# A hybrid decoder layer on one core: the second stage's three-term products regrouped over four tiles, the block sums stored in another order, and 24 stores issued from GpSimd's queue

## The chip, the core and the metric

The kernel runs on one NeuronCore of one Trainium2 chip. A core has TensorE (matmul, PE in the profile; PEld is its weight load), VectorE (DVE), ScalarE (ACT), GpSimd (POOL) and SyncE (SP). SP and POOL here mainly issue DMAs: each keeps its DMAs in one order, and a DMA that has to wait for something holds up every DMA behind it on the same engine. The metric is the device time of one execution in microseconds, median over several runs; less is better. One execution is profiled, and its trace gives every instruction with its start, its length and what it waited for.

## The reference, cut to what matters

The input x is (1, 2048, 1024) in f32, and there is one layer. The first part (projection, two groups of recurrent heads) is not touched by the change; the second part is the output projection, a norm and the feed-forward network:

```python
h = _rmsnorm(x, norm1_w[l])
proj = h @ w_in[l]
...
x = x + jnp.concatenate([o_hg, o_rw], axis=-1) @ w_out[l]
x = x + _conv_ffn(_rmsnorm(x, norm2_w[l]), w_up[l], conv_w[l], conv_b[l], w_down[l])
...
return _rmsnorm(x, final_norm_w)

def _conv_ffn(h, w_up, conv_w, conv_b, w_down):
    u = h @ w_up                                  # 1024 -> 2 * 2816
    u = <causal depthwise convolution, 3 taps>(u) + conv_b
    gate, val = jnp.split(u, 2, axis=-1)
    return (jax.nn.silu(gate) * val) @ w_down     # 2816 -> 1024
```

## The kernel before

**Three terms for one product.** Every large product is made at near-f32 precision from two halves. `split` (L241 to L248) rounds a tile to its high part on ScalarE (L246, names that end in h) and subtracts to get the low part on VectorE (L247, names that end in l); `split_to` (L239, L240) does the same into given tiles. `mm3` (L259 to L264) then adds three matmuls into one PSUM accumulator: high by high (L262), high by low (L263) and low by high (L264), each 128x128 by 128x512. Their lines tell the three terms apart in the trace. The program's names in a row stand as output, then moving operand, then stationary operand: `ua<-Bh,uwl` is the low part of a weight tile, stationary, with the high part of a B tile streaming through.

**Second stage, in order of time.** It runs from about 1391 us to the end.

1. The last block's output projection. For each half `dh` of the 1024 columns, eight k tiles in the order 0, 1, 4, 5, 2, 3, 6, 7 are multiplied into four accumulators `wacc`, one for each 128 rows. For k tile n, `weights` loads and splits a tile of w_out (names `uraw`, `woh`, `wol`) and `take` loads and splits the tile of the heads' output (into slices of `Bh` and `Bl`); then four `mm3`.
2. The up-projection, `run`. The feature columns are 22 blocks of 128 for gate and for value (`NFF` = 22) and the 2048 positions two halves, so that n goes from 0 to 43. Each n computes a 2x2 block product by Strassen's scheme with seven products; each product (`prod`) is four k tiles by three terms, 12 matmuls. The accumulators are `ua`, `ub` and `ud`, the B operands are seven pairs `Bh[i]`, `Bl[i]` that stay in SBUF for one half, and the weight operands are loaded raw (`uraw`), combined on VectorE (`s`) and split (`uwh`, `uwl`). After n the convolution and the gate are computed on VectorE and ScalarE (`cg`, `cv`, `y`) and the result goes to DRAM tensors `gd` (L1449): to gd_154 and gd_155 for the first half, to gd_156 and gd_157 for the second.
3. One side job after each product. `aside` (one call for each of the seven products of an n) pops a list that was filled ahead: `norm_last` (the norm and the transposes of the last blocks, L1253 and L256), sums of B tiles (`Ts`) and of down weights (`Tw`), and `sums(g, kk)`. `sums` loads four `gd` tiles in four slots of a ring of six (`br`, L1124), combines them with four additions on VectorE (L1293) and stores the four results to `Sg` (L1294). For g = 0 it runs at n = 23 to 33 on gd_154 and gd_155; for g = 1 with kk < 7 it runs at n = 36 to 42 on gd_156 and gd_157, while those tensors are still being written.
4. Between the halves (n = 21 and 22) the seven B pairs are rebuilt for the second half (`rebuild`, `build`), and eleven steps of an independent product (`between`, accumulators `fa`) are placed between the others to keep TensorE fed.
5. The down-projection, again by Strassen: 2 groups g, 7 products p, 11 k steps each. `down_start` does five steps, and the last loop does the others. Step s loads two raw tiles four steps ahead (`draw`, L1462, ring of six), splits them two steps ahead (`dah`, `dal`, `dbh`, `dbl`) and does four `mm3` (`d_matmuls`) into `da` or `db`. At four steps (13, 19, 25 and 31) `g_sums` makes the four sums of g = 1 that `sums` did not make: four loads `sraw`, four operations (L195 to L198), four stores to `Sg` (L201). At the end of a product `evict` adds it to the residual tile, and `finish` scales a finished tile and stores it to the output.

**What sets the order.** The program is written as above, and a tile framework then puts each engine's instructions into an order by its own estimates, with semaphores for the dependences. It follows a DRAM tensor as one object: a load from gd_157 waits for the stores to gd_157 that stand ahead of it, whichever rows they write.

Of the kernel before, what the change touches and what calls it, by code (L numbers as in the profile page):

```python
# [18 lines left out]
P = 128  # L19
T = 2048  # L20
D = 1024
KD = D // P
# [39 lines left out]
def tile_layer(ctx, tc, consts, x, norm1_w, w_in, hg_lb_logits, hg_norm_w, rw_shift_mu, rw_w0, rw_w2,  # L62
# [5 lines left out]
    dma = nc.sync.dma_start  # L68
# [124 lines left out]
    def g_sums(tile_, g, kk):  # L193

        a11, a12, a21, a22 = (tile_(krows(gd_[2 * g + u], q, kk)) for u in range(2) for q in range(2))  # L195
        V.tensor_add(a22, a21, a22)
        V.tensor_sub(a21, a11, a21)
        V.tensor_sub(a11, a22, a11)  # L198
        V.tensor_sub(a12, a12, a11)
        for i, t_ in enumerate((a22, a11, a21, a12)):  # L200
            dma(krows(Sg[g][i], 0, kk), t_)  # L201
# [7 lines left out]
    def d_loads(s_, tile_):  # L209
# [3 lines left out]
                tile_(krows(Tw[b], 0, kk) if isinstance(b, int) else wd_quarter(*b, kk)))  # L213

# [45 lines left out]
    def mm3(acc, lhs, rhs, first, last, skip=False):  # L260
# [3 lines left out]
        TE.matmul(acc, ll, rh, start=False, stop=last, skip_group_check=skip)  # L264

# [843 lines left out]
    with ExitStack() as c2:  # L1109
# [36 lines left out]
        with tc.tile_pool(name="op", bufs=1, reuse_waits="tile") as op_:  # L1146
# [84 lines left out]
        with tc.tile_pool(name="up", bufs=1, reuse_waits="tile") as up:  # L1231
# [11 lines left out]
            def norm_last(b, i2):  # L1243
# [17 lines left out]
                aside_of([load, None, lambda: scale(0), lambda: scale(1), None] + [lambda: next(g)] * KD)  # L1261
# [25 lines left out]
            def sums(g, kk):  # L1287

                ts = []
                ops = ((3, V.tensor_add, 2, 3), (2, V.tensor_sub, 0, 2), (0, V.tensor_sub, 3, 0), (1, V.tensor_sub, 1, 0))  # L1290
# [5 lines left out]
                aside_of([lambda: ts.extend(raw_(krows(gd_[2 * g + u], q, kk)) for u, q in QB), None, None]  # L1296
# [15 lines left out]
            def down_start():  # L1312

                accs = [pst("da") for _ in range(4)]
                for s_ in range(DS):
                    lhs, rhs = (split(uw, t_, [P, BLK], "uw", 5) for t_ in d_loads(s_, raw_))
                    for i in range(4):
                        d_matmuls(accs, s_, lhs, rhs, i)
                dstate["accs"] = accs

            def between():

                accs = [pst("fa") for _ in range(4)]
                for kk in range(KH):
                    lhs, rhs = (split(uw, raw_(v), [P, BLK], "uw", 5)
                                for v in (krows(gd_[0], 1, kk), wd_quarter(1, 0, kk)))
                    for i in range(4):
                        mm3(accs[i], [t_[:, i * P:(i + 1) * P] for t_ in lhs], rhs, kk == 0, kk == KH - 1, True)
# [16 lines left out]
            def run():  # L1345
# [9 lines left out]
                for n in range(2 * NFF + 1):  # L1355
                    h, fb = n // NFF, n % NFF
                    if n < 2 * NFF:
# [7 lines left out]
                        def prod(acc, nm, bi, first, n=n, ops=ops):  # L1365
# [89 lines left out]
    with tc.tile_pool(name="dn", bufs=1, reuse_waits="tile") as dn:  # L1455
# [33 lines left out]
        def finish(g, u, i):  # L1489
# [3 lines left out]
            dma(out[0, t0:t0 + P, :], t_)  # L1493
# [23 lines left out]
        for s_ in range(DS, N):  # L1517
# [6 lines left out]
            if s_ < N - 3:  # L1524
                lhs, rhs = ops.pop(s_)
                for i in range(4):
# [52 lines left out]
```

## Time and profile before

| | |
|---|---|
| median of 3 runs | 2740.66 us (2735.97 to 2741.07) |
| profiled execution | 2734.05 us |
| its span in the trace | 2732.2 us |
| TensorE busy | 2631.2 us, 96% of the span, 18059 matmuls |
| VectorE busy | 1896.6 us, 69% |
| ScalarE busy | 1348.1 us, 49% |
| GpSimd busy | 367.5 us, 13% |
| mean granted TensorE clock | 0.991 |

The profiled execution is 6.6 us faster than the median; the span is what the trace covers, and 1.85 us of the execution lie outside it. A row of a timeline gives the start and the length in us, the engine, the line, the operation, out<-in, the shape, and in brackets the idle time ahead of it with what ended that. Matmuls overlap: one starts 0.227 us after the other though each lasts 0.39, so that a lost stretch shows in the starts or as bracketed idle time. A row of the groups gives the count, then busy time and mean ns of one, then the idle time just ahead with what ended it. A row of the windows gives the length, and for PE, PEld, DVE, ACT and POOL the busy time with the number of instructions, then the granted clock, the DMA engines' busy share and GB/s.

### The profile page before, as it was taken

How to read it: one execution, taken by the hardware profiler on the slowest of the kernel's cores; microseconds unless marked ns; L12 is line 12 of the kernel's file. 1: busy time of each engine (PE TensorE's matmuls, PEld its weight loads, DVE VectorE, ACT ScalarE, POOL GpSimd, SP SyncE). 2: the span in 40 equal slices, each digit the busy share in tenths (PEclk: the TensorE clock that was granted, in tenths of full speed). 3: DMA queues.
4: the chain of work that ended last, by engine and by line, in shares of the span. 5: the costliest groups of instructions: out<-in, count | busy, mean ns of one | idle time of the engine just before them, and what ended most of it. 6: DMA issues, size and time to landing. Idle time of an engine off the chain costs nothing.

```text
span 2732.2 us, 47983 instructions
## 1 busy us (share of the span) xinstructions
PE 2631.2 (96%) x18059; PEld 2097.0 (77%) x18059; DVE 1896.6 (69%) x3665; ACT 1348.1 (49%) x2168; POOL 367.5 (13%) x660
## 2 busy tenths in 40 slices
PE   7989999989999999999899999999999999999998
PEld 5767777767777767777677788887888877788887
DVE  4856656566456654756668789988888888677556
ACT  4546443444544335334456765456555445445444
POOL 6433222212321113222100000000000000000000
PEclk9999999999999999999999999999999999999999
DMA  8655544354663546854576358746655454898665
GB/s 299 198 162 165 171 138 134 115 147 156 215 199 105 138 140 212 280 143 132 165 245 192 119 193 268 234 151 222 222 187 194 132 191 131 287 320 289 213 193 185
DMA packets 365438, 517.88 MB, mean 190 GB/s; under 512 B 97439, under 2 KB 194069, under 8 KB 365205
## 3 DMA queue, kind: packets, MB, share of 16 engines
q1 hardware_dynamic: 313265, 345.39, 39.4%
q0 software_dynamic: 51872, 169.41, 19.2%
q8 instruction: 142, 2.33, 0.4%
q14 instruction: 91, 0.75, 0.1%
q10 hardware_dynamic: 68, 0.02, 0.0%
HBM read 376.27 MB, written 138.41 MB: 188 GB/s over the span
## 4 chain that ended last, share of the span: by engine, by line
PE 68%; DVE 11%; DMA 9%; issue 6%; ACT 4%; SPq 1%; POOL 1%; DVEq 0%; ACTq 0%; POOLq 0%
PE pj L262 8%; PE pj L263 7%; PE pj L264 7%; PE ua L262 4%; PE ua L264 4%; PE ua L263 4%; PE da L262 3%; PE da L263 3%; PE da L264 3%; PE ud L264 2%; PE ud L262 2%; PE ud L263 2%; PE db L263 2%; PE db L262 2%; PE db L264 2%
## 5 line engine op out<-in xcount | busy, mean ns | idle before, releaser
L262 PE MATMUL pj<-hh,wh 128*128 128x512 f32 x960 | 402.7, 420 | 2.2 <-ACT rkv L117 1.1
L263 PE MATMUL pj<-hl,wh 128*128 128x512 f32 x960 | 378.4, 394 | 0.0
L264 PE MATMUL pj<-hh,wl 128*128 128x512 f32 x960 | 378.4, 394 | 0.0
L262 PE MATMUL ua<-Bh,uwh 128*128 128x512 f32 x704 | 276.7, 393 | 7.2 <-ACT m L117 5.6
L264 PE MATMUL ua<-Bh,uwl 128*128 128x512 f32 x704 | 274.4, 390 | 0.0
L263 PE MATMUL ua<-Bl,uwh 128*128 128x512 f32 x704 | 274.2, 389 | 0.0
L262 PEld LDWEIGHTS pj<-hh,wh 128*128 128x128 f32 x960 | 181.0, 189 | 55.6 <-issue 12.2
L264 PEld LDWEIGHTS pj<-hh,wl 128*128 128x128 f32 x960 | 181.0, 189 | 40.1 <-DMA wl<-Win170l 0.6
L263 PEld LDWEIGHTS pj<-hl,wh 128*128 128x128 f32 x960 | 181.4, 189 | 39.1 <-issue 6.2
L246 ACT CAST uwh<-uraw 128x512 fp32r<-128x512 f32 x220 | 134.5, 617 | 139.3 <-PE ua L263 61.8
L247 DVE TENSOR_TENSOR dal<-draw,dah 128x512 fp32r<-128x512 f32 x138 | 95.3, 690 | 112.5 <-ACT dah L246 112.3
L247 DVE TENSOR_TENSOR uwl<-uraw,uwh 128x512 fp32r<-128x512 f32 x220 | 147.1, 686 | 36.3 <-ACT uwh L246 36.3
L246 ACT CAST dah<-draw 128x512 fp32r<-128x512 f32 x138 | 85.8, 622 | 166.2 <-PE da L263 74.5
L262 PEld LDWEIGHTS ua<-Bh,uwh 128*128 128x128 f32 x704 | 132.2, 188 | 37.4 <-ACT m L117 8.9
L264 PEld LDWEIGHTS ua<-Bh,uwl 128*128 128x128 f32 x704 | 132.1, 188 | 28.2 <-DVE uwl L247 0.4
L263 PEld LDWEIGHTS ua<-Bl,uwh 128*128 128x128 f32 x704 | 132.3, 188 | 26.7
L262 PE MATMUL ud<-Bh,uwh 128*128 128x512 f32 x352 | 137.7, 391 | 0.0
L264 PE MATMUL ud<-Bh,uwl 128*128 128x512 f32 x352 | 137.1, 389 | 0.0
L263 PE MATMUL ud<-Bl,uwh 128*128 128x512 f32 x352 | 137.0, 389 | 0.0
L263 PE MATMUL da<-dbl,dah 128*128 128x512 f32 x332 | 129.5, 390 | 0.2 <-DVE dbl L247 0.2
L264 PE MATMUL da<-dbh,dal 128*128 128x512 f32 x332 | 129.2, 389 | 0.0
L1449 POOL DMA_DIRECT2D gd<-y x2 | 1.1, 554 | 952.0 <-DVE y L1447 952.0
(567 smaller groups left out, 6189.3 us busy)
## 6 DMA issues: line engine op xcount, KB each, us to landing
uraw<-in_w_up_dram SPq DMA_DIRECT2D x176, 256.0 KB, 3.3
woraw<-in_w_out_dram POOLq DMA_DIRECT2D x96, 256.0 KB, 3.5
br<-gd SPq DMA_DIRECT2D x88, 256.0 KB, 4.4
draw<-Sg SPq DMA_DIRECT2D x88, 256.0 KB, 3.3
draw<-Tw SPq DMA_DIRECT2D x88, 256.0 KB, 3.4
gd<-y SPq DMA_DIRECT2D x86, 256.0 KB, 2.9
Sg<-br SPq DMA_DIRECT2D x72, 256.0 KB, 2.3
xt<-x1d SPq DMA_DIRECT2D x32, 512.0 KB, 6.5
```

What stands on the lines that cost most here:

```text
L246: S.copy(hi, src)
L247: V.tensor_sub(lo, src, hi.bitcast(F32))
L262: TE.matmul(acc, lh, rh, start=first, stop=False, skip_group_check=skip)
L263: TE.matmul(acc, lh, rl, start=False, stop=False, skip_group_check=skip)
L264: TE.matmul(acc, ll, rh, start=False, stop=last, skip_group_check=skip)
L1449: (dma if end is None else nc.gpsimd.dma_start)(gd_[2 * h + b][fb * P:(fb + 1) * P, :], ys[0][:, b * BLK:(b + 1) * BLK])
```

## The change

Four things change, all in the second stage. The instruction order of all engines is the same in both programs up to the first `wacc` matmul.

**Terms.** A new function does the first term of four tiles, then the second term of the four, then the third:

```diff
+    def terms3(jobs, first, last):
+
+        for j in range(3):
+            for n, (acc, (lh, ll), (rh, rl)) in enumerate(jobs):
+                TE.matmul(acc, *((lh, rh), (lh, rl), (ll, rh))[j], start=first(n) and j == 0, stop=last(n) and j == 2,
+                          skip_group_check=True)
```

It takes the place of four `mm3` in the up products, in `between`, in `down_start`, in the down steps other than the last k step of a product and the last three steps of all, and in the first two k tiles of each half of the output projection:

```diff
-                    for i in range(4):
-                        is_ = slice(i * P, (i + 1) * P)
-                        mm3(accs[i], (ohl[k][0][:, is_], ohl[k][1][:, is_]), w, n == 0, n == KD - 1)
+                    prods = [(accs[i], [t_[:, i * P:(i + 1) * P] for t_ in ohl[k]], w) for i in range(4)]
+                    if n < 2:
+                        terms3(prods, lambda i: n == 0, lambda i: False)
+                    else:
+                        for p_ in prods:
+                            mm3(*p_, False, n == KD - 1, True)
...
-                            for k in range(4):
-                                mm3(acc, (wh[:, k, :], wl[:, k, :]), (bh[:, k, :], bl[:, k, :]),
-                                    first and k == 0, k == 3, True)
+                            terms3([(acc, (wh[:, k, :], wl[:, k, :]), (bh[:, k, :], bl[:, k, :])) for k in range(4)],
+                                   lambda k: first and k == 0, lambda k: k == 3)
...
-                for i in range(4):
-                    d_matmuls(acc, s_, lhs, rhs, i)
-                    if kk == KH - 1:
+                if kk < KH - 1:
+                    d_step(acc, s_, lhs, rhs)
+                else:
+                    for i in range(4):
+                        d_matmuls(acc, s_, lhs, rhs, i)
                         evict(g, p, accs, i)
```

**Sums.** The four tiles are loaded second pair first, and the operations overwrite them in such a way that the results stand in the order in which they are stored. The values are the same sums.

```diff
-                ops = ((3, V.tensor_add, 2, 3), (2, V.tensor_sub, 0, 2), (0, V.tensor_sub, 3, 0), (1, V.tensor_sub, 1, 0))
+                ops = ((1, V.tensor_add, 0, 1), (0, V.tensor_sub, 2, 0), (2, V.tensor_sub, 1, 2), (3, V.tensor_sub, 3, 2))
...
-                aside_of([lambda: ts.extend(raw_(krows(gd_[2 * g + u], q, kk)) for u, q in QB), None, None]
+                aside_of([lambda: ts.extend(raw_(krows(gd_[2 * g + u], q, kk)) for u, q in QB[2:] + QB[:2]), None, None]
```

**The norm's side job** has one more empty slot between the scaling and the transposes:

```diff
-                aside_of([load, None, lambda: scale(0), lambda: scale(1), None] + [lambda: next(g)] * KD)
+                aside_of([load, None, lambda: scale(0), lambda: scale(1), None, None] + [lambda: next(g)] * KD)
```

**Stores.** The 16 stores of `g_sums` and the 8 output stores of g = 0 are issued by GpSimd's queue instead of SP's; the output stores of g = 1 stay on SP:

```diff
+    dma, store = nc.sync.dma_start, nc.gpsimd.dma_start
...
-            dma(krows(Sg[g][i], 0, kk), t_)
+            store(krows(Sg[g][i], 0, kk), t_)
...
-            dma(out[0, t0:t0 + P, :], t_)
+            (dma if g else store)(out[0, t0:t0 + P, :], t_)
```

In the changed program the lines lie further down: a matmul of `terms3` is L275, `split` is at L251 and L252, the load of `raw_` at L1136, the sums at L1308 and L1309, the store to `gd` at L1462, the loads of the down stage at L1475.

**How the order of the instructions moves.** First, SP's DMAs during one n of the sums for g = 1 (n = 36 to 42). gd_156 and gd_157 are the second half's two activation tensors, Sg_162 to Sg_165 the four sums. Before:

```order
L1141 DMA uraw<-in_w_up_dram 128x4x128
L1124 DMA br<-gd_156 128x512
L1124 DMA br<-gd_157 128x512 x2
L1294 DMA Sg_165<-br 128x512
L1124 DMA br<-gd_156 128x512
L1294 DMA Sg_162<-br 128x512
L1294 DMA Sg_164<-br 128x512
L1141 DMA uraw<-in_w_up_dram 128x4x128
L1294 DMA Sg_163<-br 128x512
L1141 DMA uraw<-in_w_up_dram 128x4x128 x2
L1449 DMA gd_156<-y_22370 128x512
L1449 DMA gd_157<-y_22370 128x512
```

and now:

```order
L1153 DMA uraw<-in_w_up_dram 128x4x128
L1136 DMA br<-gd_157 128x512
L1136 DMA br<-gd_156 128x512 x2
L1136 DMA br<-gd_157 128x512
L1309 DMA Sg_162<-br 128x512
L1309 DMA Sg_164<-br 128x512
L1309 DMA Sg_163<-br 128x512
L1309 DMA Sg_165<-br 128x512
L1153 DMA uraw<-in_w_up_dram 128x4x128 x3
L1462 DMA gd_156<-y_22368 128x512
L1462 DMA gd_157<-y_22368 128x512
```

In both lists the first three loads belong to the sums at hand and the fourth is already the first of the next n. The first of the four operations needs the two tiles of gd_157. Before, these were the second and the third load behind the stores to `gd`, and the store of the preceding sums' last tile (Sg_165) stood ahead of the fourth load. Now the one tile of gd_157 has come an n earlier and the other is the first load behind the stores to `gd`; it waits for the store to gd_157, the later of the two, and all four stores of the sums stand behind the loads. Second, VectorE at the same place. Before:

```order
L1421 TENSOR_TENSOR cv<-ud,m_22640 128x512
L1293 TENSOR_TENSOR br<-br 128x512
L1438 COPY cg<-halo 128x2
L1438 COPY cv<-halo 128x2
L247 TENSOR_TENSOR uwl<-s_22754,uwh 128x512
L1293 TENSOR_TENSOR br<-br 128x512 x2
L247 TENSOR_TENSOR uwl<-uraw,uwh 128x512
L1293 TENSOR_TENSOR br<-br 128x512
L1441 SCALAR_TENSOR_TENSOR y_22717<-cv,cvt,y_22717 128x1024
```

and now:

```order
L1434 TENSOR_TENSOR cv<-ud,m_21956 128x512
L1451 COPY cg<-halo 128x2
L1451 COPY cv<-halo 128x2
L252 TENSOR_TENSOR uwl<-s_22068,uwh 128x512
L1308 TENSOR_TENSOR br<-br 128x512 x4
L252 TENSOR_TENSOR uwl<-uraw,uwh 128x512
L1454 SCALAR_TENSOR_TENSOR y_22031<-cv,cvt,y_22031 128x1024
```

The four sums of an n now stand in one piece; before, the last of the preceding n's sums stood ahead of the copies, and the third and last of its own n behind one more split. Third, SP's DMAs around the first `g_sums` of the down stage. Before:

```order
L1462 DMA sraw<-gd_156 128x512 x2
L1462 DMA sraw<-gd_157 128x512 x2
L1462 DMA draw<-Sg_159 128x512
L1462 DMA draw<-Tw_167 128x512
L1477 DMA xt_23623<-x1d_147 128x1024
L201 DMA Sg_162<-sraw 128x512
L201 DMA Sg_163<-sraw 128x512
L201 DMA Sg_164<-sraw 128x512
L201 DMA Sg_165<-sraw 128x512
L1462 DMA draw<-Sg_159 128x512
L1462 DMA draw<-Tw_167 128x512
```

and now:

```order
L1475 DMA sraw<-gd_156 128x512 x2
L1475 DMA sraw<-gd_157 128x512 x2
L1475 DMA draw<-Sg_159 128x512
L1475 DMA draw<-Tw_167 128x512
L1490 DMA xt_23621<-x1d_147 128x1024
L1475 DMA draw<-Sg_159 128x512
L1475 DMA draw<-Tw_167 128x512
```

The next step's two loads no longer stand behind the four stores; the stores are the same four on GpSimd's queue, where only the later `g_sums` stores and the eight output stores follow them.

More of the change, by code (lines that the diff above doesn't have):

```diff
@@ L213, in d_loads, with d_step @@
                 tile_(krows(Tw[b], 0, kk) if isinstance(b, int) else wd_quarter(*b, kk)))
+    def d_step(accs, s_, lhs, rhs):
+        g, p, kk = steps[s_]
+        terms3([(accs[i], [t_[:, i * P:(i + 1) * P] for t_ in lhs], rhs) for i in range(4)],
+               lambda i: kk == 0 and p in (0, 1, 3), lambda i: False)
     def d_matmuls(accs, s_, lhs, rhs, i):
```

8 lines of the change are left out of this document (3 added, 5 removed).

## The prediction

> **What bounds the kernel now.** I read the page's head first, then the groups of instructions by line, then windows of two like stretches, then timelines at the places where TensorE waits.
>
> ```profile
> span 2732.2 us, 47983 instructions
> PE 2631.2 (96%) x18059; PEld 2097.0 (77%) x18059; DVE 1896.6 (69%) x3665; ACT 1348.1 (49%) x2168; POOL 367.5 (13%) x660
> L262 PE MATMUL ua<-Bh,uwh 128*128 128x512 f32 x704 | 276.7, 393 | 7.2 <-ACT m L117 5.6
> L264 PE MATMUL ua<-Bh,uwl 128*128 128x512 f32 x704 | 274.4, 390 | 0.0
> L262 PE MATMUL da<-dbh,dah 128*128 128x512 f32 x332 | 126.0, 390 | 2.4 <-ACT dbh L246 2.4
> L263 PE MATMUL fa<-uwl,uwh 128*128 128x512 f32 x44 | 17.4, 394 | 2.6 <-DVE uwl L247 2.6
> L262 PE MATMUL fa<-uwh 128*128 128x512 f32 x44 | 15.0, 392 | 0.8 <-ACT uwh L246 0.8
> ```
>
> TensorE sets the end. In the second stage its groups stand idle for a few us in all: the up products 7.2 at the first term and nothing at the low parts, the steps between the halves 2.6 and 0.8, the down products 2.4. The change can win these and little else, unless a matmul itself becomes cheaper or dearer. The rate of a dense stretch answers that:
>
> ```profile
> 2499.74 0.39 PE L263 MATMUL db<-dbl,dah 128*128 128x512 f32 x1
> 2499.96 0.39 PE L264 MATMUL db<-dbh,dal 128*128 128x512 f32 x1
> 2500.19 0.39 PE L262 MATMUL db<-dbh,dah 128*128 128x512 f32 x1
> ```
>
> L263 keeps the stationary tile of the matmul ahead of it, L264 takes another, the next L262 another again and a new accumulator as well; the starts are 0.22 and 0.23 us apart all the same, and every matmul has its weight load (18059 of each). The new order changes the stationary tile at every matmul and the accumulator too; at this rate that costs nothing. So the change is worth what its waits are worth, and I take it place by place.
>
> **A, the start of the output projection.** The first k tile's low parts come late.
>
> ```profile
> 1391.48 0.40 PE L262 MATMUL wacc<-woh,Bh 128*128 128x512 f32 x1
> 1393.02 0.50 PE L263 MATMUL wacc<-wol,Bh 128*128 128x512 f32 x1 [1.15 <-DVE wol L240]
> 1394.83 0.50 PE L264 MATMUL wacc<-woh,Bl 128*128 128x512 f32 x1 [1.30 <-DVE Bl L240]
> 1396.12 0.63 PE L262 MATMUL wacc<-woh,Bh 128*128 128x512 f32 x1
> ...
> 1391.00:1395.10 4.10, 1.65 (x6) 0.83 (x5) 4.10 (x7) 0.74 (x2) 0.49 (x1) 1.00 0.71 263
> 1395.10:1399.00 3.90, 3.90 (x11) 3.04 (x11) 0.88 (x2) 0.00 (x0) 0.00 (x0) 0.56 0.93 237
> ...
> 1455.09 0.50 PE L262 MATMUL ua<-Bh,uwh 128*128 128x512 f32 x1 [1.46 <-ACT uwh L246]
> ```
>
> One matmul waits for the low weight, the next for the low part of the other operand (VectorE is busy for all 4.10 us), and behind them nine more of the first k tile are left. In the new order four high matmuls run from 1391.48, four with the low weight from 1393.02, and only four are left at 1394.83. VectorE's order here is the same in both, so these two times stay. Before, ten matmuls of this k tile start at 1394.83 or later (that one and nine behind it), now four: 6 x 0.227 = 1.36 us. In addition the granted clock fell to 0.56 in the next 3.9 us, when eleven matmuls took what seventeen take at 0.227: up to 1.4 us more if the fuller start keeps the clock up. On the other side stands the wait of 1.46 us at the first up product, for a weight tile whose load need not move with it: what arrives there early may wait there longer. Ends 0 and 2.8, I take 1.5.
>
> [...]
>
> **B, the norm's transposes.** One empty slot more moves the transposes of each `norm_last` by one product, 12 x 0.227 = 2.7 us.
>
> ```profile
> 1556.38 0.55 PE L256 MATMUL tp<-ident,xt 128*128 128x128 f32 x3 [0.96 <-DVE xt L1253]
> ```
>
> The tile came 0.96 us too late, so one product hides it whole. No work is added, the tile's two buffers are held 2.7 us longer. Between 0.3 and 1.0; I take 1.0.
>
> **C, between the halves.** Here low parts are late, and the new order does four high matmuls, then the neighbour's four high and two to four low ones, before the first low one of `fa`.
>
> ```profile
> 1865.13 0.50 PE L263 MATMUL fa<-uwl,uwh 128*128 128x512 f32 x1 [1.00 <-DVE uwl L247]
> 1900.80 0.50 PE L263 MATMUL fa<-uwl,uwh 128*128 128x512 f32 x1 [1.62 <-DVE uwl L247]
> ```
>
> Four to six more matmuls of cover are 0.9 to 1.4 us at each of the two, up to 2.4 together, and the 0.8 at the high part is not helped. Against it, a B tile that is to be rebuilt is now read last by the ninth matmul of its product instead of the third: 6 x 0.227 = 1.36 us later for the first k tile, and ScalarE, which rebuilds it, does its work in order, the next split behind it. One or two such delays cancel the gain. From -2 to +2.4; I take 0.7.
>
> **D, the sums of g = 1.** The like stretch of the sums of g = 0 stands first, one n of each.
>
> ```profile
> 2012.30:2031.35 19.05, 19.05 (x86) 15.78 (x85) 17.09 (x26) 9.69 (x14) 0.00 (x0) 1.00 0.59 191
> 2208.61:2229.44 20.83, 19.36 (x84) 15.69 (x84) 17.08 (x26) 9.46 (x16) 0.00 (x0) 1.00 0.54 176
> DVE br L1293 <- DMA br<-gd: 23.9, 8, 3.7
> 2206.20 0.81 SPq L1449 DMA_DIRECT2D gd<-y  x2
> 2208.61 0.38 SPq L1141 DMA_DIRECT2D uraw<-in_w_up_dram  x1
> 2209.09 1.41 SPq L1124 DMA_DIRECT2D br<-gd  x3
> 2215.45 1.42 DVE L1293 TENSOR_TENSOR br<-br 128x512 f32<-128x512 f32 x2 [3.72 <-DMA br<-gd]
> DMA to landing us min/median/max: 2.0/3.8/5.3
> ```
>
> For g = 0 an n takes TensorE's 84 matmuls, 19.05 us; VectorE has 17.09 us of work in it and 1.96 to spare. For g = 1 VectorE has the same work and waits 3.72 us for a load, which is 1.76 more than it has: the n takes 20.83, 1.78 longer. Over the group it waits 23.9 us in 8 waits, 3.0 each, of which about 1.0 is over what it can spare; for seven n that is 7.1 us, near the 7.2 of the up group. This is a stretch where VectorE and a chain of transfers (store of `y`, load, sum) set the pace, not TensorE.
>
> The tile that ends the wait is the third load of the three at 2209.09, issued at about 2210.1, landed 5.3 us later. In the new order the first operation needs the first of the three, which has to follow the store to gd_157, 0.4 us behind the other: issue 2209.5, landing 3.8 at most (the median of loads and stores alike), so 2213.3. The second needs the next load, issued 0.5 us behind and slower than the first; the fourth needs the third. VectorE comes there 0.6 us earlier, at 2211.1, as the preceding n's last sum no longer stands ahead. It waits 2.2 us for the first load and 0.6 to 0.9 more for the second: about 2.8 to 3.1 in place of 3.7. The chain is shortened, not removed, because a load still stands behind the store just issued. 0.6 us for seven n is 4.2; the others' waits are shorter than this one, 3.0 to 3.7, so I take 3.4. Ends: 0, if the loads land as late as before, and 7.1.
>
> **E, the down stage's stores.** The four stores of the first `g_sums` wait for VectorE, and the next loads stand behind them on SP.
>
> ```profile
> 2374.57 0.32 SPq L1477 DMA_DIRECT2D xt<-x1d  x1
> 2378.75 2.98 SPq L201 DMA_DIRECT2D Sg<-sraw  x4
> 2381.84 0.39 SPq L1462 DMA_DIRECT2D draw<-Sg  x1
> 2385.25 0.62 ACT L246 CAST dah<-draw 128x512 fp32r<-128x512 f32 x1 [5.26 <-DMA draw<-Sg]
> 2386.66 1.20 PE L262 MATMUL da<-dbh,dah 128*128 128x512 f32 x4 [2.44 <-ACT dbh L246]
> 2375.98 0.69 DVE L247 TENSOR_TENSOR dbl<-draw,dbh 128x512 fp32r<-128x512 f32 x1
> ```
>
> The pair of loads left at 2381.84, its first tile was split at 2385.25, 3.4 us later, and the matmul started 1.4 after that, 2.44 late. Without the stores ahead, the pair leaves when its ring slots come free, with the split that ends at 2376.7: five us earlier. Even at the 5.3 that a slow load took above, the matmul's operands are there at 2376.7 + 5.3 + 1.4 = 2383.4, and TensorE is free at 2384.2. So the whole 2.4 goes; the other three `g_sums` show no such wait, and the group's 2.4 says the same. On GpSimd's queue the stores delay nothing, since it has nothing else to do in this stage, and the `Sg` tiles they write are first read over 60 steps of 12 matmuls later. The eight output stores of g = 0 are taken from SP where TensorE waits for nothing: 0. Ends 1.5 and 2.4.
>
> **Sum.** 1.5 + 1.0 + 0.7 + 3.4 + 2.4 = 9.0 us off the profiled execution: 2734.05 - 9.0 = 2725.1. That execution lies 6.6 us under the median of the runs shown, so off the median: 2740.66 - 9.0 = 2731.7 us.
>
> **Rivals.** What a measurement here can tell from no change is 0.2%, 5.5 us.
>
> 1. *The gains stay short of the end.* A is used up at the wait of 1455.09, the loads of D land no earlier since they still follow the store, and C's cover is paid back by the rebuilds. B and E stay: 3.4 us, 2737.3. For it: D's chain of store and load is still there. Against: the first load of three now decides, not the third.
> 2. *D's wait goes below what VectorE can spare.* Then the 7.1 comes whole: 9.0 - 3.4 + 7.1 = 12.7, 2728.0. For it: the median landing of 3.8. Against: three loads together took up to 5.3.
> 3. *The sums in one piece make VectorE the bound for g = 0 too.* Four sums in a row stop VectorE until the last tile is there, and all splits behind them stop as well. If its wait there became the 3.0 of g = 1, each of the eleven n would take 17.09 + 3.0 = 20.1 in place of 19.05: 11.4 us, and D would give nothing. It decides from a wait of 1.96 us per n. Sum: 11.4 - 5.6 = 5.8 us slower, 2746.5. Against: gd_154 and gd_155 are finished then, so no load stands behind a fresh store, and all the waits of the row are eight, as many as g = 1 needs alone.
>
> **How the numbers follow.** The forecast has 0.48, rival 1 0.26, rival 2 0.14, rival 3 0.12. The forecast's own range is 2728 to 2735. The range of 8 in 10 reaches to rival 2 with the spread of the runs below it (2722) and over rival 1 to near the median before and a little past it (2743), with most of rival 3 left out. Faster by over 5.5 us: nearly all of rival 2, 0.13, and nine tenths of the forecast, 0.43, and a little of rival 1, 0.02: 0.58. Slower by over 5.5: half of rival 3 and mishaps in C, 0.10. Within: 0.32.
>
> **What would show it.** A: the second k tile's first matmul 1.4 to 2.8 us earlier, and the granted clock of 1395 to 1399 near 1. B: no idle time at L256. C: the groups of `fa` idle for under 2 us in all. D: the windows of n = 36 to 42 nearer 20.2 than 20.8, VectorE's wait at L1308 near 2.4 on average and ended by two loads, and no wait there for g = 0. E: the group `da` idle 0. The forecast is wrong if the dense starts move from 0.227 us, if idle time appears in g = 0, or if a first up product waits longer by what A won.

## The result, and the profile after

The changed kernel takes 2732.29 us in the median of 22 runs (2717.2 to 2740.99), the kernel before 2739.46 us in 22 runs beside it (2731.65 to 2753.36). The ratio is 0.9966, with a 95% interval of 0.9953 to 0.9979: faster by 0.34%, 9 us (the two medians alone are 7.2 apart). The forecast was 2731.7 us, and 9.0 us less than before.

The head of the page of the changed kernel, and its groups by line that answer to those of before (count | busy us, mean ns | idle time ahead of the group and what ended it):

```profile
span 2728.8 us, 47991 instructions
PE 2633.8 (97%) x18059; PEld 2098.7 (77%) x18059; DVE 1898.3 (70%) x3665; ACT 1357.3 (50%) x2166; POOL 380.4 (14%) x684
L275 PE MATMUL ua<-Bh,uwh 128*128 128x512 f32 x704 | 191.5, 394 | 6.6 <-ACT m L117 6.3 <-ACT uwh L251 0.3
L275 PE MATMUL da<-dbh,dah 128*128 128x512 f32 x300 | 81.7, 390 | 0.0
L261 PE MATMUL tp<-ident,xt 128*128 128x128 f32 x64 | 12.2, 272 | 0.0
L275 PE MATMUL fa<-uwl,uwh 128*128 128x512 f32 x44 | 12.0, 395 | 2.8 <-DVE uwl L252 2.8
L275 PE MATMUL fa<-uwh 128*128 128x512 f32 x44 | 11.9, 392 | 2.1 <-ACT uwh L251 2.1
```

The mean length of a matmul has not moved (389 to 395 ns), as the dense stretch had said. The idle time of the down group (`da`, 2.4 before) and of the transposes (`tp`, 1.0) is gone. That of the groups between the halves (`fa`) has grown from 3.4 to 4.9, and the up group still waits 6.6 us, 6.3 of them for `m`, ScalarE's copy of an accumulator. So something that made that group wait is gone and something else has come.

Totals hide this, and one execution hides more: the first stage, with the same instructions in the same order, took 1380.6 us in the profile of before and 1368.7 to 1386.7 in those of the experiments. So I cut the second stage at fixed matmuls and compare place by place. The times are the distances between the starts of the first matmuls of these places: "n = 12 to 19" runs from the first `ub` matmul of n = 12 to that of n = 20, "down 1" takes 1200 matmuls from the 61st of `da` on, the output projection and "n = 0 to 2" meet at the first `ua` matmul, and the whole ends with the start of the last matmul. Each kernel was profiled twice (the second time with only a comment changed):

| place | before | before, again | changed | changed, again |
|---|---|---|---|---|
| first stage | 1380.6 | 1385.2 | 1381.8 | 1386.7 |
| output projection | 48.4 | 49.7 | 46.4 | 46.9 |
| n = 0 to 2 | 63.9 | 62.1 | 64.1 | 64.8 |
| n = 3 to 11 (transposes) | 178.9 | 178.7 | 177.9 | 177.4 |
| n = 12 to 19 (down-weight sums) | 152.7 | 152.9 | 157.3 | 156.7 |
| n = 20 to 23 (between the halves) | 110.4 | 114.2 | 111.9 | 112.1 |
| n = 24 to 34 | 209.4 | 209.4 | 209.4 | 209.4 |
| n = 35 to 42 (sums of g = 1) | 159.8 | 160.1 | 155.5 | 154.2 |
| n = 43 and the first five down steps | 30.1 | 30.1 | 30.0 | 30.0 |
| down 1 | 276.1 | 278.7 | 272.9 | 272.8 |
| rest of the down stage | 103.1 | 103.1 | 103.2 | 103.2 |
| second stage in all | 1332.9 | 1339.0 | 1328.5 | 1327.5 |

The mean of the second stage falls from 1335.9 to 1328.0, by 7.9 us, near the 9 that were timed. Four places win, as forecast. One loses 4.2 us that the prediction did not have at all, and n = 0 to 2 is longer by 1.4.

### The profile page after: what moved, and what is told of

The parts are those of the page before. It is cut to its first block, busy times and chain, and to the rows that moved or that the text cites. A ratio compares the mean times of both kernels' runs of the same rounds, so it can differ in the third digit from the quotient of the medians.

```text
span 2728.8 us, 47991 instructions
## 1 busy us (share of the span) xinstructions
PE 2633.8 (97%) x18059; PEld 2098.7 (77%) x18059; DVE 1898.3 (70%) x3665; ACT 1357.3 (50%) x2166; POOL 380.4 (14%) x684
## 4 chain that ended last, share of the span: by engine, by line
PE 72%; DMA 8%; DVE 8%; issue 6%; ACT 4%; SPq 1%; POOL 1%; DVEq 0%; ACTq 0%; POOLq 0%
PE ua L275 14%; PE pj L267 8%; PE pj L268 7%; PE pj L269 7%; PE da L275 7%; PE ud L275 7%; PE db L275 5%; PE ub L275 3%; PE hg L985 2%; DMA woraw<-in_w_out_dram 1%; PE rw L721 1%; DVE uwl L252 1%; DMA TZ<-T0d 1%; PE rw L901 1%; DVE y L1454 1%
## 5 line engine op out<-in xcount | busy, mean ns | idle before, releaser
L275 PE MATMUL ua<-Bh,uwh 128*128 128x512 f32 x704 | 191.5, 394 | 6.6 <-ACT m L117 6.3
L275 PE MATMUL ua<-Bl,uwh 128*128 128x512 f32 x704 | 188.4, 389 | 0.0
L275 PE MATMUL ua<-Bh,uwl 128*128 128x512 f32 x704 | 188.4, 389 | 0.0
L251 ACT CAST uwh<-uraw 128x512 fp32r<-128x512 f32 x220 | 134.1, 617 | 92.2 <-PE ua L275 62.7
L252 DVE TENSOR_TENSOR dal<-draw,dah 128x512 fp32r<-128x512 f32 x138 | 95.3, 690 | 110.1 <-PE da L275 50.8
L252 DVE TENSOR_TENSOR uwl<-uraw,uwh 128x512 fp32r<-128x512 f32 x220 | 147.6, 687 | 33.7 <-PE ua L275 19.2
L275 PEld LDWEIGHTS ua<-Bh,uwh 128*128 128x128 f32 x704 | 129.9, 188 | 37.0 <-ACT m L117 10.8
L251 ACT CAST dah<-draw 128x512 fp32r<-128x512 f32 x138 | 85.7, 621 | 138.2 <-PE da L275 51.7
L275 PEld LDWEIGHTS ua<-Bl,uwh 128*128 128x128 f32 x704 | 132.1, 188 | 28.0
L275 PEld LDWEIGHTS ua<-Bh,uwl 128*128 128x128 f32 x704 | 132.1, 188 | 27.9
L1462 POOL DMA_DIRECT2D gd<-y x2 | 1.1, 554 | 950.3 <-DVE y L1460 950.3
L251 ACT CAST wh<-woraw 128x512 fp32r<-128x512 f32 x96 | 59.0, 618 | 108.8 <-DMA woraw<-in_w_out_dram 54.0
L252 DVE TENSOR_TENSOR dbl<-draw,dbh 128x512 fp32r<-128x512 f32 x138 | 94.9, 688 | 16.7 <-ACT dbh L251 16.3
L251 ACT CAST dbh<-draw 128x512 fp32r<-128x512 f32 x138 | 86.0, 623 | 39.8 <-PE da L275 12.7
L316 DVE SCALAR_TENSOR_TENSOR rkv<-pj,vt,rkv 128x511 f32<-128x511 f32 x48 | 35.9, 748 | 100.3 <-ACT rkv L117 100.3
L251 ACT CAST uwh<-s 128x512 fp32r<-128x512 f32 x88 | 53.5, 620 | 102.2 <-DVE s L1356 72.0
```

Of the source, the lines that this page charges most:

```text
L251: S.copy(hi, src)
L252: V.tensor_sub(lo, src, hi.bitcast(F32))
L275: TE.matmul(acc, *((lh, rh), (lh, rl), (ll, rh))[j], start=first(n) and j == 0, stop=last(n) and j == 2, skip_group_check=True)
L316: V.scalar_tensor_tensor(y[:, 1:], acc[:, :BLK - 1], mu, y[:, 1:], ALU.mult, ALU.add)
L1462: (dma if end is None else nc.gpsimd.dma_start)(gd_[2 * h + b][fb * P:(fb + 1) * P, :], ys[0][:, b * BLK:(b + 1) * BLK])
```

## Two places read closely

**The output projection (A).** The timeline of TensorE in the changed kernel, and the window that answers to the one in which the clock had fallen (its columns as before; the 1.00 ahead of the DMA share is the granted clock):

```profile
1392.44 1.08 PE L275 MATMUL wacc<-woh,Bh 128*128 128x512 f32 x4
1393.99 1.20 PE L275 MATMUL wacc<-wol,Bh 128*128 128x512 f32 x4 [0.46 <-DVE wol L245]
1395.79 1.20 PE L275 MATMUL wacc<-woh,Bl 128*128 128x512 f32 x4 [0.61 <-DVE Bl L245]
1396.83 0.39 PE L275 MATMUL wacc<-woh,Bh 128*128 128x512 f32 x1
...
1396.00:1400.00 4.00, 4.00 (x18) 3.28 (x18) 0.94 (x2) 0.06 (x1) 0.00 (x0) 1.00 0.89 250
```

The two waits are 0.46 and 0.61 us in place of 1.15 and 1.30, and the next four microseconds hold 18 matmuls at full clock, against eleven at 0.56. This is what the forecast called its upper bound. The second k tile starts 4.4 us after the first matmul, against 7.2 before. Of these 2.8 us some 0.8 are given back at the third and fourth k tile, where the splits are now the later ones; 2.0 stay. The granted clock was 0.56 behind the waits of 1.15 and 1.30 us (1395.10 to 1399.00 before) and 1.00 behind those of 0.46 and 0.61; the last section sets longer waits beside these.

**The down-weight sums (n = 12 to 19), the loss that was not forecast.** Rows of TensorE, ScalarE, VectorE and SP of the changed kernel, from the effect back to the cause, and two rows of its waits (total, times, longest). The last two rows are SP's in the kernel before, at the same place:

```profile
1755.39 1.19 PE L275 MATMUL ua<-Bh,uwh 128*128 128x512 f32 x4 [2.27 <-ACT m L117]
1754.22 0.62 ACT L251 CAST uwh<-s 128x512 fp32r<-128x512 f32 x1 [3.25 <-DVE s L1356]
1740.83 0.69 DVE L1287 TENSOR_TENSOR br<-br 128x512 f32<-128x512 f32 x1 [3.28 <-DMA br<-in_w_down_dram]
1736.83 1.07 SPq L1282 DMA_DIRECT2D Tw<-br  x2
1737.99 1.10 SPq L1136 DMA_DIRECT2D br<-in_w_down_dram  x1
DVE br L1287 <- DMA br<-in_w_down_dram: 3.9, 2, 3.3
DVE br L1288 <- DMA br<-in_w_down_dram: 4.0, 2, 2.2
...
1741.46 3.75 SPq L1124 DMA_DIRECT2D br<-in_w_down_dram  x5
1752.97 4.74 SPq L1267 DMA_DIRECT2D Tw<-br  x4
```

TensorE waits for ScalarE's copy `m`, which stands behind a cast, which waits for a weight sum `s` on VectorE. VectorE has no gap from 1740.8 on; it is late because it stood 3.28 us at L1287, the first subtraction of a down-weight sum, whose load SP had queued among the stores of the preceding sum. Before, the loads and the four stores went out in one piece each. Nothing in the diff touches this code. But these sums are later entries of the list from which the norm's transposes come too, and the extra empty slot, four times, moved each of them by four products.

## The experiments

The timed ratios below have intervals of 0.14 to 0.21% to each side, 4 to 6 us, so they tell 9 us from nothing but not 4 from 7. Each verdict therefore rests on the places of the trace, and the ratio stands beside it.

### The changed kernel once more

> The changed kernel once more, only a comment differs. Compared place by place (time from one milestone of TensorE's stream to the next): against the profile of before, the changed kernel's profile won 2.0 us in the output projection, 1.0 at the norm's transposes, 4.4 in the sums of g = 1 and 3.2 in the down stage, and lost 4.6 us at n = 12 to 19 (sums of the down weights) and 1.5 between the halves (n = 20 to 23). Theory 1 (the order makes the loss): n = 12 to 19 shows some 4 to 5 us of waits again, and the total is 7 to 9 us below before. Rival (one execution's slow transfers): those waits are gone, under 1 us, and this profile lies 4 us lower.

Measured: 0.9963 (0.9949 to 0.9978). The last column of the table above: n = 12 to 19 loses 4 us again. The loss is in the order and not one execution's slow transfers.

### The slot undone

```diff
-                aside_of([load, None, lambda: scale(0), lambda: scale(1), None, None] + [lambda: next(g)] * KD)
+                aside_of([load, None, lambda: scale(0), lambda: scale(1), None] + [lambda: next(g)] * KD)
```

> The changed kernel with the norm's extra empty slot taken out again. Theory 1: the slot, four times in all, pushes every later side job of the list by four products, so the sums of the down weights land at another place of each n, behind VectorE's convolution work; without it n = 12 to 19 is back at 0.3 us of waits (from 4.8), the transposes get their 1.0 to 1.4 us wait back, and the kernel is 3 to 4 us faster than the changed one. Rival 1 (the regrouped terms make that loss): n = 12 to 19 keeps 4 to 5 us, and the kernel is 1 us slower than the changed one. Rival 2 (chance): under 1 us there, as in the repeat.

Measured: 0.9955 (0.9937 to 0.9973). n = 12 to 19 takes 152.3 us, with no wait left; n = 3 to 11 takes 179.4, 1.5 to 2 more than with the slot. So the slot wins what was forecast at the transposes and, with the rest of the change, loses 4.4 to 4.9 later on. The second stage takes 1324.6 us, 3 to 4 less than the changed kernel's.

### The three terms tile by tile again

```diff
-        for j in range(3):
-            for n, (acc, (lh, ll), (rh, rl)) in enumerate(jobs):
+        for n, (acc, (lh, ll), (rh, rl)) in enumerate(jobs):
+            for j in range(3):
```

> The changed kernel with the three terms tile by tile again everywhere; the sums, the slot and the stores stay changed. Theory 1 (the terms only matter where low parts come late): the output projection loses its 2.0 us, the places D and E keep their 4.4 and 3.2, the loss of 4.6 at n = 12 to 19 stays, n = 20 to 23 goes back by 0 to 1.5. In all 0 to 2 us slower than the changed kernel. Rival (the regrouping holds weight and B tiles longer, and that makes the losses): n = 12 to 19 and n = 20 to 23 are back at 0.3 and 4.2 us of waits, and the kernel is 4 us faster than the changed one.

Measured: 0.996 (0.9939 to 0.9981). The output projection is back at 48.4 us, D and E keep their gains (155.4 and 272.8). n = 12 to 19 takes 152.3: with the slot still in. That is the rival's figure, and it fell in a way neither theory had: taking away either the slot or the regrouping removes the whole loss. The second stage takes 1323.3 us, 4 to 5 less than the changed kernel's.

### Only the up products tile by tile

```diff
-                            terms3([(acc, (wh[:, k, :], wl[:, k, :]), (bh[:, k, :], bl[:, k, :])) for k in range(4)],
-                                   lambda k: first and k == 0, lambda k: k == 3)
+                            for k in range(4):
+                                mm3(acc, (wh[:, k, :], wl[:, k, :]), (bh[:, k, :], bl[:, k, :]),
+                                    first and k == 0, k == 3, True)
```

> The changed kernel with the up products alone tile by tile again; the step products between the halves, the down steps and the output projection stay regrouped. Theory 1: the output projection keeps its 2.0 us, n = 12 to 19 keeps its loss of 4.6 us (it is the slot's), n = 20 to 23 is within 1 us of the changed kernel. Rival (the up products' regrouping makes the losses): n = 12 to 19 back at 0.3 us of waits and n = 20 to 23 at 4 us, the kernel 5 us faster than the changed one.

Measured: 0.9965 (0.995 to 0.998). n = 12 to 19 takes 152.3 us, so of the regrouping it is that of the up products. n = 20 to 23 did not improve: 114.6 us, and n = 0 to 2 took 67.3. Both places vary between executions (below), so I read nothing from these two. The second stage takes 1331.1 us, 2.6 to 3.6 more than the changed kernel's, so the rival's gain of 5 us in all did not come: the 4.4 to 4.9 won at n = 12 to 19 went at these two places and in "down 1" (274.9).

### The old order of the sums' loads

```diff
+                ops = ((3, V.tensor_add, 2, 3), (2, V.tensor_sub, 0, 2), (0, V.tensor_sub, 3, 0), (1, V.tensor_sub, 1, 0))
...
-                aside_of([lambda: ts.extend(raw_(krows(gd_[2 * g + u], q, kk)) for u, q in QB[2:] + QB[:2]), None, None]
+                aside_of([lambda: ts.extend(raw_(krows(gd_[2 * g + u], q, kk)) for u, q in QB), None, None]
```

> The changed kernel with the sums' loads in the old order (first pair first) and the operations that belong to it. Theory (D as forecast: the first operation waits for the third load of the old order and for the first of the new): the stretch n = 35 to 42, 154.2 to 155.5 us in the two executions of the changed kernel, goes back to 159 to 160, VectorE's wait for the loads from 1.6 us each to about 3; 4 to 5 us slower than the changed kernel there, and the gains in the output projection and the down stage stay. Rival (the gain of D comes from the regrouped terms or from the stores on the other queue): the stretch stays at 154 to 156.

Measured: 0.9976 (0.9959 to 0.9992). n = 35 to 42 goes back to 159.0 us and seven waits of 3.1 us, and the other gains stay. D is the order of the loads, with the order of VectorE's sums that the framework makes from it. The four operations are the same ones on the same data under other names.

### The stores back on SP

```diff
-    dma, store = nc.sync.dma_start, nc.gpsimd.dma_start
+    dma, store = nc.sync.dma_start, nc.sync.dma_start
```

> The changed kernel with the 24 stores back on SP's queue. Theory (E as forecast: the pair of loads stands behind the four stores): the first 1200 matmuls of the down stage go from 272.8 us back to 275 to 276.5, with one wait of 2 to 2.6 us on ScalarE's split; everything ahead of it as in the changed kernel. Rival (the regrouped down steps removed that wait): they stay at 272.8 to 273.

Measured: 0.9984 (0.9967 to 1.0). "Down 1" takes 281.5 us, 8.7 more than the changed kernel and 5.4 more than the first profile of before. SP's DMAs and TensorE in this kernel:

```profile
2369.43 0.32 SPq L1490 DMA_DIRECT2D xt<-x1d  x1
2373.73 2.98 SPq L201 DMA_DIRECT2D Sg<-sraw  x4
2376.80 0.41 SPq L1475 DMA_DIRECT2D draw<-Sg  x1
...
2381.28 1.20 PE L275 MATMUL da<-dbh,dah 128*128 128x512 f32 x4 [2.15 <-ACT dbh L251]
...
2452.61 1.30 PE L275 MATMUL da<-dbh,dah 128*128 128x512 f32 x2 [2.62 <-DVE xt L1500]
```

The pair of loads stands behind the four stores again, and TensorE waits 2.15 us where it had waited 2.44. A second wait of 2.62 comes at the end of a product, where VectorE's additions stand behind splits of tiles that came late; before had none there. Behind that second wait the matmuls at 2454.56 and 2454.99 start 0.43 us apart and take 0.63 each, where those ahead of it (2447.10 to 2449.60) start 0.227 apart and take 0.39; this is a part of the rest of the 8.7, of which the two waits are 4.8. In this order the stores on SP cost more than the forecast's one wait.

### The stores alone

The same two lines of `store` put into the kernel before, and nothing else.

> The kernel before with the 24 stores on GpSimd's queue and nothing else changed. Theory (E as forecast, by itself): the first 1200 matmuls of the down stage go from 276.1 to 272.8 us (the changed kernel's value), all else as before, 3 us faster in all, ratio 0.9988. Rival (E needs the regrouped steps): 275 or more.

Measured: 0.9976 (0.9961 to 0.9992). "Down 1" takes 273.2 us, 2.9 to 5.5 less than in the two profiles of before. E stands by itself. Its other places are those of before (n = 35 to 42: 160.3; n = 12 to 19: 152.3).

### Loads of rows stored long before

```diff
-                aside_of([lambda: ts.extend(raw_(krows(gd_[2 * g + u], q, kk)) for u, q in QB), None, None]
+                aside_of([lambda: ts.extend(raw_(krows(gd_[2 * g + u], 0 if g else q, kk)) for u, q in QB), None, None]
```

This stands on the kernel with the old order of the loads.

> The changed kernel with the old order of the sums' loads, and for g = 1 the loads of the second half of the rows replaced by the same loads from the first half, which were stored long before (so the sums of g = 1 are of other rows). Same bytes, same instructions. Theory (D's wait is the chain of a store of fresh rows, a load of these rows, and the sum): with the old order, which had 159.0 us for n = 35 to 42 and seven waits of 3.1 us, it falls to 152.4 to 153 and VectorE waits under 0.5 us. Rival (the loads are late because of the ring's slots or the queue): it stays over 157.

Measured: 0.9965 (0.9946 to 0.9984). n = 35 to 42 takes 152.3 us, the 672 matmuls' own time. The group of the sums there:

```profile
L1308 DVE TENSOR_TENSOR br<-br 128x512 f32<-128x512 f32 x72 | 49.4, 686 | 0.5
```

It waits 0.5 us in all 72, with the same bytes and the same ring. So the wait of D comes from the chain of store, load and sum over fresh rows. The framework also moved the loads: they now leave 8 us and more behind the pair of stores to `gd`, in place of some 3, and most of an n ahead of their sums. So the run shows that the fresh rows force the chain; what the ring and the queue would cost at the old places it does not show.

### The slot kept, the later jobs put back in place

```diff
-            def four(srcs, make, dsts):
+            def four(srcs, make, dsts, rest=(None,)):
...
-                          lambda: make(ts, 0), lambda: (make(ts, 1), [dma(d, t_) for d, t_ in dsts(ts)]), None])
+                          lambda: make(ts, 0), lambda: (make(ts, 1), [dma(d, t_) for d, t_ in dsts(ts)]), *rest])
...
-                four([hsrc(1, q, b, kk) for q, b in QB], t_make, t_out(lambda i, kk=kk: tdst(1, i, kk)))
+                four([hsrc(1, q, b, kk) for q, b in QB], t_make, t_out(lambda i, kk=kk: tdst(1, i, kk)), ())
```

> The changed kernel with the norm's extra slot kept, and the four side jobs that follow it (the Ts sums) without their last empty slot, so that every sum of the down weights runs at the product at which it ran before. Theory 1 (the slot's loss is that the later jobs are shifted): n = 3 to 11 keeps the changed kernel's 2.1 us of waits, n = 12 to 19 falls from 4.2 to 4.8 to under 0.5, 4 us faster in all. Rival (four more products of delay are not the cause; the regrouped up products starve VectorE or SP there in any alignment): n = 12 to 19 stays over 3.

Measured: 0.9954 (0.9939 to 0.9969). n = 3 to 11 keeps 177.4 us and n = 12 to 19 takes 152.3, without a wait. The alignment of the down-weight sums with the rest of an n is the cause, and it can be mended for nothing. The second stage takes 1323.7 us.

### The regrouping in the output projection alone

The up products, the steps between the halves and the down steps go tile by tile; sums, slot and stores as changed.

> The changed kernel with the regrouped terms in the output projection's first two k tiles alone; up products, steps between the halves and down steps go tile by tile; sums, slot and stores as changed. Theory (of the regrouping only the output projection's start gains anything): output projection 46.2 to 46.9 us as in the changed kernel (48.4 with no regrouping), n = 12 to 19 without waits, n = 20 to 23 with 4 to 5 us of waits, 35 to 42 at 154 to 155.5, down stage 272.8; the second stage in all about 1321.5 us, 6 to 7 less than the changed kernel, a ratio to before of 0.994. Rival (the regrouping also gains between the halves or in the down steps): n = 20 to 23 over 6 us of waits or the down stage over 274.

Measured: 0.9964 (0.9946 to 0.9982), 2726.92 us against 2738.58. The places are as expected: 46.4, n = 12 to 19 at 152.3, n = 20 to 23 at 110.4, n = 35 to 42 at 154.2, "down 1" 272.8; the second stage takes 1321.0 us, the shortest of all. Its timed gain does not show more than the changed kernel's, and the expected ratio of 0.994 lies just outside its interval. Whether it or the kernel with the realigned jobs beats the changed one is not settled by these intervals.

### All sums of g = 1 in the down stage

```diff
-    EARLY = 7
+    EARLY = 0
```

This stands on the kernel of the experiment above.

> The kernel with the regrouping in the output projection alone, and in addition all eleven sums of g = 1 made in the down stage by g_sums (EARLY = 0 in place of 7), none at n = 36 to 42. Theory (D's remaining waits come from these sums, VectorE having 17.1 us of work in 19.05): the stretch n = 35 to 42 has no wait, 152.4 us, 1.7 less than with the new load order; the down stage, whose stores now go by the other queue, takes the seven more for at most 1 us. Second stage about 1319.5 us, against 1321.0. Rival (each g_sums costs the down stage a wait, as the first one did for 2.4 us in the kernel before): the down stage 4 us or more longer, and the kernel slower than the one without.

Measured: 0.9982 (0.9965 to 0.9999). n = 35 to 42 falls to 152.3 us as the theory had it, but "down 1" takes 286.7, 13.9 more. The rival holds. The down stage's longest waits in this kernel:

```profile
DVE sraw L196 <- DMA sraw<-gd: 19.5, 8, 5.8
PE da L267 <- DVE xt L1501: 6.8, 1, 6.8
```

VectorE stands up to 5.8 us at the first addition of a `g_sums`, with splits and the residual additions behind it, and TensorE waits 6.8 us for its accumulators. So here the loads that VectorE waited for were paid for by what stood behind them; the one wait of TensorE is half of the 13.9 us.

### The kernel before once more

> The kernel before once more, only a comment differs. Over the ten variants the timed gain is on average some 4 to 5 us larger than the difference of the second stages of the profiles, all of which stand against one profile of before (second stage 1332.9 us). Theory (that one execution of before was a good one): this profile's second stage is longer, 1335 to 1339 us, above all where it waited least by chance, n = 0 to 2, 12 to 19 and 20 to 23; D and E, which are set by the order, repeat at 159 to 160.5 and 275.5 to 277. Rival (the difference lies in the first stage, whose length varies by 18 us with the same instructions): the second stage repeats within 1 us. The timed ratio is 1.000 within its interval either way.

Measured: 0.9999 (0.9982 to 1.0016), the null as it should be. The second stage takes 1339.0 us, 6.1 more than in the first profile; D and E repeat (160.1, with eight waits of 3.05 us; a wait of 2.46 against 2.44). Of n = 0 to 2, 12 to 19 and 20 to 23, where it was expected to be longer, only the last is (114.2); the rest lies in the output projection and in "down 1". A part of this is the clock: its mean over the whole execution was 0.986, against 0.991 in the first profile, and in the down stage it was 0.50 for 3.4 us. At n = 22 a wait took 3.21 us that was 1.62 in the first profile. The same wait of the down stage as in the prediction, with the window behind it:

```profile
2395.60 2.08 PE L262 MATMUL da<-dbh,dah 128*128 128x512 f32 x4 [2.46 <-ACT dbh L246]
2397.48 0.63 PE L263 MATMUL da<-dbl,dah 128*128 128x512 f32 x1
...
2395.60:2399.00 3.40, 3.40 (x8) 2.72 (x9) 2.05 (x5) 1.86 (x4) 0.00 (x0) 0.50 0.90 337
```

In the first profile four matmuls behind the wait took 1.20 us, here 2.08: the granted clock is 0.50 for 3.4 us, in which eight matmuls run, in place of 1.00 and fifteen. The same wait costs 2.6 us in one execution and 4.3 in another.

## Why the prediction was right, term by term

| term | forecast | measured (mean of the two profiles of each, unless said) |
|---|---|---|
| A, output projection | -1.5 | -2.4 |
| B, transposes | -1.0 | -1.1 |
| down-weight sums | not there | +4.2 |
| C, between the halves | -0.7 | -0.3, within the spread of 3.8 |
| D, sums of g = 1 | -3.4 | -5.1 |
| E, down stage | -2.4 | -4.6 |
| n = 0 to 2 | 0 | +1.4, varies by as much between executions |
| sum | -9.0 | -7.9 |

The sum was right, but in part by luck: a loss of 4.2 us that was left out is balanced by two gains, D and E, that were set 1.7 and 2.2 too small.

**A** came as described at its place, and the clock's share, of which the forecast had allowed a little, came whole (1.00 in place of 0.56). But waits at the up products just behind it, of which the prediction had set the first against it, took more than half back. The output projection and n = 0 to 2 together took 111.2 to 112.3 us in the four profiles with the old start, and 109.7 to 111.6 in eight of the ten with the new one: on average 1.1 less, a little under the 1.5. In the other two (the old up products, and `EARLY` = 0) the two places took 114.3 and 113.9; in the first of these the first up product waited 2.59 us. That wait alone does not account for it: it was 2.22 us in the changed kernel's second profile too, against 1.46 in the first profile of before and no more than 0.3 in its second.

**D**: the term of 4.2 us, seven times 0.6, was scaled down to 3.4 for the milder waits, which was wrong: the old order of the loads costs 4.2 (159.0 against the changed kernels' 154.8), and the two profiles of before lie another microsecond higher. In place of 3.7 the sum now waits 2.66, for the first load:

```profile
2208.09 0.81 SPq L1462 DMA_DIRECT2D gd<-y  x2
2211.57 2.83 SPq L1136 DMA_DIRECT2D br<-gd  x4
2215.68 2.87 DVE L1308 TENSOR_TENSOR br<-br 128x512 f32<-128x512 f32 x4 [2.66 <-DMA br<-gd]
DVE br L1308 <- DMA br<-gd: 16.1, 10, 2.7
```

The load leaves 3.5 us behind the pair of stores and its tile is there 4.1 later, and the four sums follow in one piece. Of the 16.1 us, 0.8 are two short waits of g = 0. The rest over seven n is 2.2, which is 0.2 more than VectorE can spare; 3.2 and 1.9 us are left of the 7 in the two profiles. The prediction's "nearer 20.2 than 20.8" (19.0 to 20.3 here) and "2.4 on average" held. Its second wait of 0.6 to 0.9 for the next load did not come at this n and came at one of the seven in the first profile; the first wait was longer than its 2.2 instead. It also misread the row of eight waits as those of g = 1 alone: one of them, 1.91 us at 1927.28, is of g = 0, and the seven of g = 1 are 22.0 us, 3.1 each.

**E**: its wait was priced with what one execution showed, 2.4 us. It was a mis-sized term: against the first profile of before the place wins 3.2, and the same wait costs 1.6 more where the granted clock was 0.50 behind it, as in the second. After the change the pairs leave SP without the stores, and GpSimd issues these at 0.54 us each:

```profile
2373.74 0.32 SPq L1490 DMA_DIRECT2D xt<-x1d  x1
2374.46 0.32 SPq L1475 DMA_DIRECT2D draw<-Sg  x1
2378.18 0.54 POOL L201 DMA_DIRECT2D Sg<-sraw  x1 [34.31 <-DVE sraw L196]
2378.91 0.54 POOL L201 DMA_DIRECT2D Sg<-sraw  x1 [0.18 <-issue]
```

The pair that had left at 2381.84 leaves at 2374.46, 0.7 us behind the load ahead of it; the prediction had it wait for its ring slots until 2376.7.

**B** held at its place, but its step "no work is added, the tile's two buffers are held 2.7 us longer" failed: it left out that the list is one list, and that an empty slot in one job moves all later jobs. Undoing the slot, undoing the up products' regrouping and realigning the later jobs each brought n = 12 to 19 from 157 to 152.3 us. Why it takes both is not shown in full. The framework makes the order of VectorE's and SP's instructions there; in the changed kernel's order the first subtraction of a sum twice stands ahead of the last one of the sum before (the rows above show the first of the two, L1287 at 1740.83), with the slot or the up products' regrouping undone once or not at all, and in the realigned kernel never.

**C**'s step failed too: the cover was to outweigh the later rebuilds by 0.7 us and bring the groups' idle time under 2. The three waits are now 1.20, 2.10 and 1.59 us against 1.00, 0.80 and 1.62 in the first profile of before: the wait for the high part, which the prediction took as not helped, grew by 1.3. Seven profiles with the regrouping took 111.5 to 112.8 us there and six without it 110.4 to 114.5; the latter's three higher figures come with a longest wait of `fa` of 2.4 to 3.2 us, and the three with none over 1.8, 110.4 to 111.3, lie below all seven. So the forecast gain is not there, and whether the regrouping loses here the spread leaves open.

One sentence of the description ahead of the prediction has to be taken back: that a load waits for all stores to its tensor whichever rows they write. In both kernels the seventh sum's loads leave while four stores to the same tensor are still to come, and each sum's loads stand right behind the store of just the rows they read. The framework had pulled the sums ahead of their place in the program, by more than one n, as far as their data allowed; the chain of D is a true one, which the loads of old rows confirm.

Of the rivals, the first (gains short of the end) and the second (D whole) lay on the two sides of the result. The third did not occur: n = 24 to 34 takes 209.4 to 209.7 us in every kernel but the one with EARLY = 0, where it takes 210.4.

## What to carry to other kernels

Where work is drawn from one list, an edit that shifts an entry is an edit of everything behind it: read the order of all engines there, not only at the entry. Put a DMA that must wait for computed data on a queue with no loads behind it; this alone was worth 2.9 to 5.5 us here. And compare profiles at fixed points of a stage, with each kernel profiled twice, before a difference of a few microseconds is given a cause.

## What the runs showed of the hardware that was not expected

In these traces the granted clock and the length of the wait ahead of it did not go together. Behind the wait of 2.46 us in the down stage of before's second profile it was 0.50 for 3.4 us; behind the same wait of the first profile, 2.44 us, it was 1.00 for the next 3.4 us (2386.66 to 2390.06, fifteen matmuls). It was 1.00 as well behind the wait of 2.27 us in the changed kernel's down-weight sums (1755.39 to 1758.80), and 0.56 behind the shorter ones of 1.15 and 1.30 us at the start of before's output projection. At 0.50 the matmuls started 0.427 us apart (2397.48 to 2398.76) instead of 0.227, over eight of them 1.6 us on top of the wait. What decided between the two is not shown.

The first stage's length varied from 1368.7 to 1386.7 us over the profiles with the same order of instructions, more than all that was studied here.
